# Gate-up products on DVE instead of POOL in a two-layer hybrid decoder trunk, with earlier 1/rms, separate places for weight sums and rebuilt operands spread out

## The chip, the cores and the metric

The kernel runs on one core of one Trainium2 chip. The metric is the device time of one execution in microseconds (us). Most times below come from one profiled execution.

## The reference

Two layers over x of 1024 tokens by 1024 channels, in float32. Each layer adds a token mixer (attention) and then a SwiGLU feed-forward:

```python
h = rms_norm(x, ffn_norm_g[layer])
a = einsum('bsd,df->bsf', h, w_gate)       # d 1024, f 2816
u = einsum('bsd,df->bsf', h, w_up)
x = x + einsum('bsf,fd->bsd', silu(a) * u, w_down)
```

The change touches the first half of the feed-forward alone: `silu(a) * u`.

## The kernel before

Matrix operands are split in a high part (a cast on ACT, L102) and the rest (a subtraction on DVE, L1062 for 128x512, L1055 for 128x1024), and each product is three matmuls (L1129 to L1131).

**Gate and up products.** The 22 tiles of 128 hidden columns go in pairs: 11 batches, b = 0 to 10, in each of two layers. A batch takes seven products, i = 0 to 6, in place of eight, by the Winograd form of Strassen's scheme: a 2x2 block of weights (gate and up, each in the two halves of d_model) by a 2x2 block of activations (halves of d_model, halves of the tokens). Product (b, i) below is product i of batch b. It has two halves, n = 0 and 1, one for each tile of the pair, of 12 matmuls each, so 24 matmuls a product. The left operands are weight blocks and their sums, which `sums_gate` (L1085 to L1087) and L1099 make on POOL from the loaded blocks. The right operands are `self.B[i]`.

**Banks.** Products 0 and 1 of a half add up in the same PSUM bank, as do 2 and 3, 4 and 5. In between, the partial sum is taken: after product 0 by a copy on ACT (L102), after 2 and 4 by an addition on DVE (L1155, L1161). The first matmul of product 1, 3 or 5 waits for that read. Product 6 has a bank of its own.

**What follows a product.** After (b, 5) DVE adds (L1164), ACT applies silu and POOL multiplies (L1166); after (b, 6) DVE adds (L1168) and POOL multiplies (L1169). `hidden` (L1188 to L1191, DVE) then forms the sums of hidden blocks, and SP writes seven blocks to DRAM.

**The start.** 1/rms of the tokens is known late. So batches 0, 1 and 2 (`EARLY = 3`) run products 0 and 1 before it is there, as (0,0), (0,1), (1,0), (1,1), (2,0), (2,1), and then (0,2) to (0,6), (1,2) to (1,6), (2,2) to (2,6). Their first two results are multiplied by 1/rms (`self.rt`, L1151) on DVE, and silu follows, in the step of product 2. The right operands 0 and 1 are dropped after (2,1), and rebuilt from DRAM (L1176, two blocks each after products (2,3) and (2,4)) for batch 3. Batches 3 to 10 run all seven products in order.

**Places and order.** One pool of 44 places of 128x1024 holds split operands (`sr`) and raw tiles (`sf`), another of 11 places of 128x512 the rest (`hf`, `hr`, `raw`). A new tile takes the place that was freed longest ago and waits for that place's last user. The Tile framework fixes the order of each engine's instructions when the kernel is built; each engine then runs its list in order. Operand preparation (`prep_gate`) is asked for 3 or 4 products ahead.

Of the kernel before, what the change touches and what calls it, by code (L numbers as in the profile page):

```python
# [14 lines left out]
AF = mybir.ActivationFunctionType  # L15
ALU = mybir.AluOpType
# [6 lines left out]
TH = 512  # L23
# [93 lines left out]
class Trunk:  # L117
# [960 lines left out]
    def sums_gate(self, b):  # L1078

        p = self.nc.gpsimd  # L1080
        for n in range(2):
            (a11, a21), a22 = (self.raws[b, w][n][:, 0:TH] for w in range(2)), self.raws[b, 1][n][:, TH:2 * TH]
            s1 = self.tmp[b, n] = (self.sf if b == 0 else self.hf).get()
            s1 = s1[:, 0:TH]
            p.tensor_tensor(s1, a21, a22, ALU.add)  # L1085
            p.tensor_tensor(a21, a11, a21, ALU.subtract)
            p.tensor_tensor(a11, s1, a11, ALU.subtract)  # L1087

    def prep_gate(self, b, i):
        p = self.nc.gpsimd  # L1090
        out = []
        for n in range(2):
            g = self.raws[b, 0][n]
            a11, a12 = g[:, 0:TH], g[:, TH:2 * TH]
            if i >= 2:
                u = self.raws[b, 1][n]
                a21, a22 = u[:, 0:TH], u[:, TH:2 * TH]
            if i == 5:
                p.tensor_tensor(a12, a12, a11, ALU.subtract)  # L1099
            out.append(self.split((a11, a12, a11, None, None, a12, None)[i] if i not in (3, 4, 6) else  # L1100
                                  a21 if i == 3 else self.tmp[b, n][:, 0:TH] if i == 4 else a22))
            if i == 4:
                (self.sf if b == 0 else self.hf).put(self.tmp.pop((b, n)))
            if i == 6:
                self.sf.put(g, u)
        due = 0 if (b, i) == (1, 0) else b + 1 if b + 1 < self.EARLY and i == 5 else b if b >= self.EARLY and i == 1 else None
        if due is not None:
            self.sums_gate(due)
        if b + 1 < self.EARLY and i == 3:
            self.take_raw(b + 1, (1,))  # L1110
        elif b + 1 == self.EARLY and i in (4, 6):
            self.take_raw(b + 1, (0,) if i == 4 else (1,))
        elif self.EARLY <= b < self.BATCHES - 1 and i == 1:
            self.take_raw(b + 1)
        return out

    def gate(self, b, i, W):
        nc = self.nc
        if i == 0:
            self.v[b] = [{}, {}]  # L1120
        for n in range(2):
# [12 lines left out]
            v = self.v[b][n]  # L1134
            if i == 0:
                if 0 < b < self.EARLY:
                    t = v["both"] = self.sf.get()
                    v["p"], v["s"] = t[:, 0:TH], t[:, TH:2 * TH]
                else:
                    v["hp"], v["hs"] = self.hf.get(), self.hf.get()  # L1140
                    v["p"], v["s"] = v["hp"][:], v["hs"][:]
                self.S.copy(v["p"], ps)
            elif i == 1:
                if b < self.EARLY:
                    self.S.copy(v["s"], ps)
                else:
                    self.S.activation(v["s"], ps, AF.Silu)
            elif i == 2:
                if b < self.EARLY:
                    for x in ("p", "s"):  # L1150
                        nc.vector.tensor_tensor(v[x], v[x], self.rt[:, 0:TH], ALU.mult)  # L1151
                    self.S.activation(v["s"], v["s"], AF.Silu)
                v["hu"] = self.hf.get()
                v["u"] = v["hu"][:]
                nc.vector.tensor_tensor(v["u"], ps, v["p"], ALU.add)  # L1155
            elif i == 3:
                nc.vector.tensor_tensor(v["p"], ps, v["p"], ALU.add)
            elif i == 4:
                v["hq"] = self.hf.get()
                v["q"] = v["hq"][:]  # L1160
                nc.vector.tensor_tensor(v["q"], ps, v["p"], ALU.add)  # L1161
            elif i == 5:
                u = v["u"]
                nc.vector.tensor_tensor(u, ps, u, ALU.add)  # L1164
                self.S.activation(u, u, AF.Silu)
                nc.gpsimd.tensor_tensor(u, u, v["q"], ALU.mult)  # L1166
            else:
                nc.vector.tensor_tensor(v["p"], ps, v["p"], ALU.add)  # L1168
                nc.gpsimd.tensor_tensor(v["s"], v["s"], v["p"], ALU.mult)  # L1169
        if b == self.BATCHES - 1 or i < 2 and b == self.EARLY - 1:  # L1170
            self.sr.put(*(x for hl in self.B[i] for x in hl))
            self.B[i] = []
        if b == self.EARLY - 1 and i in (3, 4):
            for m in (0, 1) if i == 3 else (2, 3):
                t = self.sf.get()
                nc.sync.dma_start(t[:], self.h_dram[m][:])  # L1176
                self.B[i - 3].append(self.split2(t))
                self.sf.put(t)
        if i == 6:
            self.hidden(b)  # L1180

    def hidden(self, b):

# [364 lines left out]
```

## Time and profile before

| what | us |
|---|---|
| median of 3 runs | 2597.59 |
| range of the 3 runs | 2596.66 to 2600.56 |
| the profiled execution | 2599.55 |
| its span in the profile | 2597.6 |
| gate-up products of layer 0, first L1129 | from 668.9 |

The page of the profile gives busy time by engine. A timeline row gives start, duration, engine, line, operation, output <- inputs, how many rows it merges, and in brackets how long the engine had been idle and what ended that. Names drop buffer numbers: `bk` is a PSUM bank, `sr` a split operand, `sf` and `hf` raw tiles, `rt` 1/rms. `x` in a row of windows is the number of instructions.

### The profile page before, as it was taken

To read this page: it belongs to the slowest core of one execution; us is meant where nothing else is said; L and a number is where in the kernel's file an instruction comes from. 1 tells how busy PE (TensorE), PEld (TensorE's weight loads), DVE (VectorE), ACT (ScalarE), POOL (GpSimd) and SP (SyncE) were. 2 spreads that over 40 slices of the span, in tenths; PEclk is the share of its full clock that TensorE was granted. 3 is DMA by queue.
4 is the path that set the end of the run, shared out by engine and by line. 5 is a ranking of instruction groups with operands and counts; after the bars stand their busy time and mean duration, and the time that the engine had idled before them with its cause. 6 is when DMAs were issued, how large, how long until landed. Compare 5 with 4: busy or idle time off the path is not lost.

```text
span 2597.6 us, 34806 instructions
## 1 busy us (share of the span) xinstructions
PE 2467.1 (95%) x11896; PEld 2021.0 (78%) x11896; DVE 1912.1 (74%) x3303; ACT 1300.8 (50%) x2618; POOL 902.3 (35%) x696
## 2 busy tenths in 40 slices
PE   8898899999989999999999999998998899999999
PEld 7786778777767888888878878876777778888887
DVE  7869958887976655589566687778779666566974
ACT  5646666764732323344456576766565233234352
POOL 4112111121264444366142232323334534443910
PEclk9999999999999999999999999999999999999999
DMA  5323142465323232374333331325531422328462
GB/s 180 91 53 82 36 102 76 116 192 169 109 90 139 96 113 102 131 266 153 111 122 75 83 100 54 98 78 135 178 136 67 150 93 98 110 74 283 126 186 82
DMA packets 148269, 307.50 MB, mean 118 GB/s; under 512 B 18515, under 2 KB 24436, under 8 KB 148092
## 3 DMA queue, kind: packets, MB, share of 16 engines
q1 hardware_dynamic: 148092, 305.28, 37.8%
q8 instruction: 93, 1.52, 0.2%
q14 instruction: 84, 0.69, 0.1%
HBM read 187.74 MB, written 75.53 MB: 101 GB/s over the span
## 4 chain that ended last, share of the span: by engine, by line
PE 64%; DVE 17%; ACT 6%; POOL 5%; issue 5%; DMA 2%; SPq 0%; DVEq 0%; POOLq 0%; ACTq 0%
PE bk L1129 8%; PE bk L1130 8%; PE bk L1131 8%; PE bk L1275 5%; PE bk L1273 5%; PE bk L1274 5%; PE bk L376 4%; PE bk L375 4%; PE bk L377 4%; PE bk L691 4%; PE bk L569 3%; DVE sf L587 3%; PE bk L677 2%; ACT sf L110 2%; DVE sr L1062 2%
## 5 line engine op out<-in xcount | busy, mean ns | idle before, releaser
L102 ACT CAST sr<-sf 128x512 fp32r<-128x512 f32 (+2 forms) x528 | 331.8, 648 | 559.0 <-PE bk L1131 189.0
L1129 PE MATMUL bk<-sr,sr 128*128 128x512 f32 x1232 | 487.8, 396 | 32.2 <-DVE hf L1155 18.0
L1062 DVE TENSOR_TENSOR sr<-sf,sr 128x512 fp32r<-128x512 f32 x430 | 411.2, 963 | 121.5 <-ACT sr L102 119.8
L1131 PE MATMUL bk<-sr,sr 128*128 128x512 f32 x1232 | 483.9, 393 | 3.4 <-DVE sr L1062 3.4
L1130 PE MATMUL bk<-sr,sr 128*128 128x512 f32 x1232 | 484.5, 393 | 0.0
L375 PE MATMUL bk<-sr,sr 128*128 128x512 f32 x768 | 308.2, 402 | 6.7 <-DVE sf L989 3.4
L376 PE MATMUL bk<-sr,sr 128*128 128x512 f32 x768 | 306.5, 399 | 2.4 <-DVE sr L932 2.3
L1129 PEld LDWEIGHTS bk<-sr,sr 128*128 128x128 f32 x1232 | 234.4, 190 | 91.9 <-DVE hf L1155 26.5
L377 PE MATMUL bk<-sr,sr 128*128 128x512 f32 x768 | 305.5, 398 | 0.0
L221 POOL TENSOR_TENSOR sr<-raw,sr 128x512 fp32r<-128x512 f32 (+2 forms) x140 | 191.3, 1383 | 305.9 <-ACT sr L102 174.9
L1131 PEld LDWEIGHTS bk<-sr,sr 128*128 128x128 f32 x1232 | 234.2, 190 | 53.6 <-DVE sr L1062 4.2
L1130 PEld LDWEIGHTS bk<-sr,sr 128*128 128x128 f32 x1232 | 234.5, 190 | 48.3
L1274 PE MATMUL bk<-sr,sr 128*128 128x512 f32 x616 | 239.7, 389 | 0.6 <-DVE sr L1062 0.6
L1273 PE MATMUL bk<-sr,sr 128*128 128x512 f32 x616 | 239.6, 389 | 0.0
L1275 PE MATMUL bk<-sr,sr 128*128 128x512 f32 x616 | 239.6, 389 | 0.0
L102 ACT CAST sr<-hf 128x512 fp32r<-128x512 f32 (+1 forms) x256 | 158.7, 620 | 135.1 <-DMA hf<-td 72.2
L569 PE MATMUL bk<-sr,sr 128*128 128x512 f32 (+2 forms) x768 | 200.4, 359 | 9.2 <-ACT sf L110 6.4
L1062 DVE TENSOR_TENSOR sr<-hf,sr 128x512 fp32r<-128x512 f32 x186 | 188.2, 1021 | 27.4 <-ACT sr L102 26.8
L691 PE MATMUL bk<-hr,sr 128*128 128x512 f32 (+2 forms) x560 | 165.5, 388 | 13.7 <-DVE hr L709 11.0
L375 PEld LDWEIGHTS bk<-sr,sr 128*128 128x128 f32 x768 | 146.1, 190 | 37.3 <-DVE sf L989 5.1
L102 ACT CAST hr<-bk 128x512 fp32r<-128x512 f32 (+2 forms) x240 | 122.5, 525 | 100.8 <-PE bk L677 88.8
L709 DVE TENSOR_TENSOR hr<-bk,hr 128x512 fp32r<-128x512 f32 (+2 forms) x240 | 142.2, 603 | 38.6 <-ACT hr L102 37.1
(203 smaller groups left out, 4917.3 us busy)
## 6 DMA issues: line engine op xcount, KB each, us to landing
hf<-td SPq DMA_DIRECT2D x146, 256.0 KB, 3.1
td<-hf SPq DMA_DIRECT2D x138, 256.0 KB, 2.0
sr<-sr SPq DMA_DIRECT2D x96, 256.0 KB, 3.6
sf<-in_wg_dram SPq DMA_DIRECT2D x44, 512.0 KB, 3.3
sf<-in_wu_dram SPq DMA_DIRECT2D x44, 512.0 KB, 3.3
sf<-in_wd_dram SPq DMA_DIRECT2D x88, 256.0 KB, 5.0
raw<-in_w_dram SPq DMA_DIRECT2D x64, 256.0 KB, 3.0
sr<-sr SPq DMA_DIRECT2D x128, 128.0 KB, 2.3
```

Of the source, the lines that this page charges most:

```text
L102: self.last = self.e.copy(out, in_)
L375: nc.tensor.matmul(ps, WH[k], hH[k], start=first and k == 0, stop=False)
L376: nc.tensor.matmul(ps, WH[k], hL[k], start=False, stop=False)
L377: nc.tensor.matmul(ps, WL[k], hH[k], start=False, stop=last and k == n - 1)
L569: nc.tensor.matmul(b[:, 0:hi - lo], r32(Q[i // 4][:, q]), r32(KK[:, lo:hi]), start=j == 0, stop=j == 1)
L1062: self.nc.vector.tensor_tensor(r32(t[:, TH:2 * TH]), x, t[:, 0:TH], ALU.subtract)
L1129: nc.tensor.matmul(ps, wh, bh, start=i in (0, 2, 4, 6) and j == 0, stop=False, skip_group_check=True)
L1130: nc.tensor.matmul(ps, wh, bl, start=False, stop=False, skip_group_check=True)
L1131: last = nc.tensor.matmul(ps, wl, bh, start=False, stop=j == 3, skip_group_check=True)
L1273: nc.tensor.matmul(ps, wh, bh, start=i in (0, 6, 2, 4) and j == 0, stop=False, skip_group_check=True)
L1274: nc.tensor.matmul(ps, wh, bl, start=False, stop=False, skip_group_check=True)
L1275: nc.tensor.matmul(ps, wl, bh, start=False, stop=j == self.PAIRS - 1, skip_group_check=True)
```

## The change

The two multiplications of `gate` move from POOL to DVE, 88 of them over both layers. The multiplication by 1/rms and the silu of the early batches become `early_r`: batch 0 keeps its step, batches 1 and 2 get it in the step of product 4 of the batch before. The sum s1 of `sums_gate` takes a place of the large pool for all early batches, where only batch 0 did. The four blocks for the right operands of batch 3 are reloaded and split one each after (2,2), (2,3), (2,4) and (2,5).

```diff
@@ sums_gate, and prep_gate where the sum is given back
-            s1 = self.tmp[b, n] = (self.sf if b == 0 else self.hf).get()
+            s1 = self.tmp[b, n] = (self.sf if b < self.EARLY else self.hf).get()
...
-                (self.sf if b == 0 else self.hf).put(self.tmp.pop((b, n)))
+                (self.sf if b < self.EARLY else self.hf).put(self.tmp.pop((b, n)))
@@ gate
             elif i == 2:
-                if b < self.EARLY:
-                    for x in ("p", "s"):
-                        nc.vector.tensor_tensor(v[x], v[x], self.rt[:, 0:TH], ALU.mult)
-                    self.S.activation(v["s"], v["s"], AF.Silu)
+                if b == 0:
+                    self.early_r(v)
...
                 self.S.activation(u, u, AF.Silu)
-                nc.gpsimd.tensor_tensor(u, u, v["q"], ALU.mult)
+                nc.vector.tensor_tensor(u, u, v["q"], ALU.mult)
             else:
                 nc.vector.tensor_tensor(v["p"], ps, v["p"], ALU.add)
-                nc.gpsimd.tensor_tensor(v["s"], v["s"], v["p"], ALU.mult)
+                nc.vector.tensor_tensor(v["s"], v["s"], v["p"], ALU.mult)
+            if i == 4 and b + 1 < self.EARLY:
+                self.early_r(self.v[b + 1][n])
...
-        if b == self.EARLY - 1 and i in (3, 4):
-            for m in (0, 1) if i == 3 else (2, 3):
-                t = self.sf.get()
-                nc.sync.dma_start(t[:], self.h_dram[m][:])
-                self.B[i - 3].append(self.split2(t))
-                self.sf.put(t)
+        if b == self.EARLY - 1 and 2 <= i < 6:
+            t = self.sf.get()
+            nc.sync.dma_start(t[:], self.h_dram[i - 2][:])
+            self.B[i // 2 - 1].append(self.split2(t))
+            self.sf.put(t)
...
+    def early_r(self, v):
+
+        for x in ("p", "s"):
+            self.nc.vector.tensor_tensor(v[x], v[x], self.rt[:, 0:TH], ALU.mult)
+        self.S.activation(v["s"], v["s"], AF.Silu)
```

In the changed kernel the lines are L1153 and L1159 (the additions after products 2 and 4), L1162 and L1166 (after 5 and 6), L1164 and L1167 (the multiplications, now on DVE), L1184 (by 1/rms) and L1193 to L1196 (`hidden`).

The built order of three places of layer 0 follows; layer 1 has the same. The number behind the first letters is the place in the pool, the one behind the underline the tile. First POOL, from the weight sums of batch 1 on (`6977` and `6981` are the two s1). Before:

```order
L1085 TENSOR_TENSOR hf0_6977<-sf40_6881 128x512
L1086 TENSOR_TENSOR sf40_6881<-sf31_6403,sf40_6881 128x512
L1087 TENSOR_TENSOR sf31_6403<-hf0_6977,sf31_6403 128x512
L1085 TENSOR_TENSOR hf1_6981<-sf36_6882 128x512
L1099 TENSOR_TENSOR sf31_6403<-sf31_6403 128x512
L1086 TENSOR_TENSOR sf36_6882<-sf29_6404,sf36_6882 128x512
L1087 TENSOR_TENSOR sf29_6404<-hf1_6981,sf29_6404 128x512
L1099 TENSOR_TENSOR sf29_6404<-sf29_6404 128x512
L1166 TENSOR_TENSOR hf2_6940<-hf2_6940,hf7_7029 128x512
L1166 TENSOR_TENSOR hf3_6957<-hf3_6957,hf8_7043 128x512
L1169 TENSOR_TENSOR hf6_6680<-hf6_6680,hf5_6679 128x512
L1085 TENSOR_TENSOR hf2_7182<-sf2_7088 128x512
```

With the change:

```order
L1085 TENSOR_TENSOR sf43_6977<-sf40_6881 128x512
L1086 TENSOR_TENSOR sf40_6881<-sf31_6403,sf40_6881 128x512
L1087 TENSOR_TENSOR sf31_6403<-sf43_6977,sf31_6403 128x512
L1099 TENSOR_TENSOR sf31_6403<-sf31_6403 128x512
L1085 TENSOR_TENSOR sf39_6981<-sf36_6882 128x512
L1086 TENSOR_TENSOR sf36_6882<-sf29_6404,sf36_6882 128x512
L1087 TENSOR_TENSOR sf29_6404<-sf39_6981,sf29_6404 128x512
L1099 TENSOR_TENSOR sf29_6404<-sf29_6404 128x512
L1085 TENSOR_TENSOR sf35_7178<-sf19_7093 128x512
L1086 TENSOR_TENSOR sf19_7093<-sf30_6407,sf19_7093 128x512
L1087 TENSOR_TENSOR sf30_6407<-sf35_7178,sf30_6407 128x512
L1099 TENSOR_TENSOR sf30_6407<-sf30_6407 128x512
```

The two POOL multiplications of batch 0 (L1166, L1166, L1169) no longer stand between the sums of batch 1 and those of batch 2; the sums of batch 2 follow at once. The first s1 lies in place 43 of the large pool, whose last reader is L1045 on DVE (`sf43_6381`), and the s1 of batch 2 in place 35, which held an operand of (0,6).

Second DVE, from the end of batch 0 (`hidden`, its last additions) to the two additions after (1,2). Before:

```order
L1062 TENSOR_TENSOR sr6_7212<-sf40_6881,sr6_7212 128x512
L1188 TENSOR_TENSOR hf7_7029<-hf2_6940,hf6_6680 128x512
L1168 TENSOR_TENSOR hf4_6694<-bk3_66,hf4_6694 128x512
L1189 TENSOR_TENSOR hf5_6679<-hf3_6957,hf7_7029 128x512
L1062 TENSOR_TENSOR sr7_7215<-sf36_6882,sr7_7215 128x512
L1191 TENSOR_TENSOR hf4_6694<-hf10_6695,hf5_6679 128x512
L1151 TENSOR_TENSOR sf10_6847<-sf10_6847,rt_145 128x512
L1155 TENSOR_TENSOR hf9_7151<-bk4_67,sf25_6761 128x512
L1062 TENSOR_TENSOR sr39_7249<-sf20_6408,sr39_7249 128x512
L1062 TENSOR_TENSOR sr35_7282<-sf22_7087,sr35_7282 128x512
L1062 TENSOR_TENSOR sr43_7246<-sf30_6407,sr43_7246 128x512
L1155 TENSOR_TENSOR hf5_7168<-bk5_68,sf28_6775 128x512
```

With the change:

```order
L1195 TENSOR_TENSOR hf1_7046<-hf3_6957,hf2_6940 128x512
L1167 TENSOR_TENSOR hf6_6680<-hf6_6680,hf5_6679 128x512
L1166 TENSOR_TENSOR hf4_6694<-bk3_66,hf4_6694 128x512
L1193 TENSOR_TENSOR hf0_7029<-hf2_6940,hf6_6680 128x512
L1167 TENSOR_TENSOR hf10_6695<-hf10_6695,hf4_6694 128x512
L1194 TENSOR_TENSOR hf5_6679<-hf3_6957,hf0_7029 128x512
L1062 TENSOR_TENSOR sr7_7175<-sf29_6404,sr7_7175 128x512
L1196 TENSOR_TENSOR hf4_6694<-hf10_6695,hf5_6679 128x512
L1153 TENSOR_TENSOR hf7_7154<-bk4_67,sf25_6761 128x512
L1062 TENSOR_TENSOR sr43_7212<-sf40_6881,sr43_7212 128x512
L1062 TENSOR_TENSOR sr39_7215<-sf36_6882,sr39_7215 128x512
L1153 TENSOR_TENSOR hf8_7168<-bk5_68,sf28_6775 128x512
```

The two multiplications (L1167) are new here, as one more is two rows ahead of the piece. A multiplication by 1/rms (L1151) and three operand splits of batch 2, which stood ahead of one or the other addition after (1,2), are gone from here; two splits of batch 1 stand between the additions instead.

Third ACT, around (3,0), whose bank 0 the copies read. Before:

```order
L102 CAST sr25_7564<-sf31_7333 128x512
L102 CAST sr28_7567<-sf40_7334 128x512
L102 CAST sr10_7570<-sf43_7423 128x512
L102 COPY hf7_7588<-bk0_63 128x512
L102 CAST sr20_7606<-hf1_7509 128x512
L102 CAST sr42_7573<-sf39_7424 128x512
```

With the change:

```order
L102 CAST sr35_7564<-sf29_7339 128x512
L102 CAST sr41_7567<-sf36_7340 128x512
L102 COPY hf1_7588<-bk0_63 128x512
L102 CAST sr39_7606<-hf10_7509 128x512
L102 CAST sr10_7570<-sf17_7423 128x512
L102 COPY hf9_7603<-bk1_64 128x512
```

The copy of the first half of (3,0) stands ahead of the cast of `7423`, which reuses a place that `hidden` of batch 2 still sends to DRAM; before, it stood behind that cast.

## Rows read from the trace of the kernel before

**Rows 1.** Page, part 1: engine, busy us, share of the span, instructions.
```profile
PE 2467.1 (95%) x11896; PEld 2021.0 (78%) x11896; DVE 1912.1 (74%) x3303; ACT 1300.8 (50%) x2618; POOL 902.3 (35%) x696
```

**Rows 2.** 50 us windows: busy us (instructions) of PE, PEld, DVE, ACT, POOL; clock; DMA.
```profile
700.00:750.00 50.00, 41.83 (x175) 33.41 (x173) 44.05 (x51) 20.29 (x33) 28.07 (x15) 0.97 0.23 74
750.00:800.00 50.00, 43.62 (x180) 34.99 (x180) 33.97 (x41) 14.79 (x22) 24.16 (x16) 0.93 0.40 138
850.00:900.00 50.00, 49.99 (x221) 41.04 (x220) 31.27 (x38) 15.17 (x26) 24.91 (x18) 1.00 0.31 112
```

**Rows 3.** Timeline of PE, layer 0: matmuls that waited; wait and releaser in brackets.
```profile
729.07 0.50 PE L1129 MATMUL bk<-sr,sr 128*128 128x512 f32 x1 [2.91 <-DVE hf L1161]
753.36 0.79 PE L1129 MATMUL bk<-sr,sr 128*128 128x512 f32 x1 [6.92 <-DVE hf L1155]
759.76 0.50 PE L1129 MATMUL bk<-sr,sr 128*128 128x512 f32 x1 [1.44 <-DVE hf L1155]
800.95 0.50 PE L1129 MATMUL bk<-sr,sr 128*128 128x512 f32 x1 [2.23 <-DVE hf L1161]
819.15 0.80 PE L1129 MATMUL bk<-sr,sr 128*128 128x512 f32 x1 [2.65 <-ACT hf L102]
```

**Rows 4.** Timeline of PE, the same matmuls in layer 1.
```profile
1993.48 0.80 PE L1129 MATMUL bk<-sr,sr 128*128 128x512 f32 x1 [2.91 <-DVE hf L1161]
2017.78 0.79 PE L1129 MATMUL bk<-sr,sr 128*128 128x512 f32 x1 [7.17 <-DVE hf L1155]
2024.18 0.50 PE L1129 MATMUL bk<-sr,sr 128*128 128x512 f32 x1 [0.91 <-DVE hf L1155]
2064.23 0.50 PE L1129 MATMUL bk<-sr,sr 128*128 128x512 f32 x1 [1.08 <-DVE hf L1161]
2080.42 0.50 PE L1129 MATMUL bk<-sr,sr 128*128 128x512 f32 x1 [2.28 <-ACT hf L102]
```

**Rows 5.** Windows of 4 us behind the wait that ends at 729.07.
```profile
728.00:732.00 4.00, 2.94 (x9) 2.34 (x10) 2.21 (x4) 1.24 (x3) 3.84 (x3) 0.78 0.00 0
732.00:736.00 4.00, 4.00 (x15) 3.18 (x15) 3.97 (x6) 3.24 (x6) 0.90 (x2) 0.79 0.00 0
```

**Rows 6.** Timeline of POOL, DVE and ACT, layer 0, ahead of 729.07.
```profile
716.74 6.87 POOL L1086 TENSOR_TENSOR sf<-sf,sf 128x512 f32<-128x512 f32 x1
...
716.63 2.34 DVE L1045 TENSOR_TENSOR sf<-sf,sf 128x1024 f32<-128x1024 f32 x2
...
722.37 1.27 DVE L1157 TENSOR_TENSOR hf<-bk,hf 128x512 f32<-128x512 f32 x2
...
726.60 1.80 DVE L1062 TENSOR_TENSOR sr<-sf,sr 128x512 fp32r<-128x512 f32 x1 [2.36 <-ACT sr L102]
...
735.10 0.63 ACT L110 ACTIVATE hf<-hf 128x512 f32<-128x512 f32 x1 [0.49 <-DVE hf L1164]
```

**Rows 7.** Timeline of DVE, layer 0, ahead of the wait that ends at 753.36.
```profile
749.30 1.73 DVE L1191 TENSOR_TENSOR hf<-hf,hf 128x512 f32<-128x512 f32 x1 [1.15 <-POOL hf L1169]
750.95 1.75 DVE L1151 TENSOR_TENSOR sf<-sf,rt 128x512 f32<-128x512 f32 x1
752.62 0.68 DVE L1155 TENSOR_TENSOR hf<-bk,sf 128x512 f32<-128x512 f32 x1
```

**Rows 8.** DVE and POOL in the down projection: two timeline rows, then a 50 us window.
```profile
1160.89 1.77 DVE L1062 TENSOR_TENSOR sr<-hf,sr 128x512 fp32r<-128x512 f32 x1
...
1160.49 1.62 POOL L1234 TENSOR_TENSOR sf<-sf,sf 128x512 f32<-128x512 f32 x1
...
1150.00:1200.00 50.00, 50.00 (x222) 41.38 (x222) 50.00 (x31) 20.13 (x37) 48.82 (x31) 1.00 0.34 102
```

**Rows 9.** Lines L1166 and L1188: count, duration ns min/median/max.
```profile
L1166 POOL TENSOR_TENSOR hf<-hf,hf x44: 1272/1296/1612, 735.8 to 2380.9; 128x512 f32<-128x512 f32 x44
...
L1188 DVE TENSOR_TENSOR hf<-hf,hf x18: 677/1226/1766, 743.9 to 2386.1; 128x512 f32<-128x512 f32 x18
```

**Rows 10.** Timeline of PE, a later batch of layer 0.
```profile
1026.53 0.50 PE L1129 MATMUL bk<-sr,sr 128*128 128x512 f32 x1 [0.32 <-DVE hf L1155]
```

## The prediction, made before the change was run

> **What bounds the kernel now.** I read the page first, then windows over the gate-up products, then the timeline of PE there, and last the queues of the engines that PE waited for. PE is busy for 95% of the span [rows 1], so only time in which it stands, or runs at less than its clock, can be won. The windows show where that is: from 850 us on 221 matmuls start in 50 us, which is 0.226 us each and 5.43 us for a product of 24; the two windows ahead of it hold 175 and 180 [rows 2]. So batches 3 to 10 run without a gap, and the early batches do not. In layer 0 five waits stand there, of 2.91, 6.92, 1.44, 2.23 and 2.65 us [rows 3], and the same five in layer 1, of 2.91, 7.17, 0.91, 1.08 and 2.28 [rows 4]. By the order of PE's matmuls the waiting ones are the first of (0,5), of (1,3) first half, of (1,3) second half, of (2,5) and of (3,1). Four of the five wait for an addition on DVE that must read a bank, the last for a copy on ACT.
>
> A wait costs more than itself where the clock falls behind it. After 729.07 the granted clock is 0.78 and 0.79 of full speed over two windows, a time at 1.2 GHz in place of 2.4; 24 matmuls take from 729.07 to 736, 6.93 us where 5.43 would do [rows 2, 3, 5]. I price a fall at 1.5 us.
>
> **What holds DVE and POOL.** Where both have additions with two inputs in SBUF queued, they take turns: 31 and 31 in 50 us, 1.61 us for a pair, while a DVE row reads 1.77 and a POOL row 1.62, waiting included [rows 8]. Alone, the same operations take 0.68 (two in a row 1.27, so 0.60 each in a stream) and 1.30 [rows 6, 9]. There is an exception, and it matters below: the POOL addition at 716.74 lasted 6.87 us, and ended 1.24 us after DVE turned to operands in PSUM at 722.37; five DVE instructions had gone ahead of it [rows 6]. The Trainium skill (SBUF — State Buffer, section "Who interferes with whom") says that a DVE instruction with two SBUF inputs contends with a GpSimd instruction that reads SBUF, and that issue order decides who blocks. The turns agree with that; the 6.87 us do not. By that rule alone the time would be my forecast; by the exception it would be the second case below.
>
> **The change part by part.**
>
> *The multiplications.* POOL loses 88 of 1.30 us, some 114 us, none of it in PE's way by itself. DVE gains 88 of 0.60, 53 us. In a batch of 7 x 5.43 = 38 us that is 2.4 us, and DVE stands twice more for a silu (0.63 on ACT, about 0.7 with the hand-over) [rows 6, 9], 3.8 us in all. DVE is busy for 31.27 of 50 us there, 14 us free a batch [rows 2], and today it also waits 1.15 us for a POOL multiplication twice a batch [rows 7]. So from batch 3 on I cost this at nothing; the cover is that idle time. If it were gone, the next addition that reads a bank would be late: one is already, by 0.32 [rows 10].
>
> *Wait at (0,5), 729.07.* The s1 of batch 1 now lies in place 43, which L1045 reads until 716.63 + 1.17 = 717.8; before, L1085 was done when L1086 was queued at 716.74. The first POOL addition to get through ends at 723.6 as before [rows 6], but it is now L1085, and L1086 and L1087 follow one addition later. DVE's split at 726.60 stands behind ACT's cast, which stands behind the cast of L1087's result. So this wait ends one POOL addition later, 1.3 us, at 730.4. In the queue of ACT the cast is also third instead of second behind L1087, 0.5 us; that falls into the same POOL addition. Bounds: nothing, if POOL gets in at 717.8 without a queue, and 1.9, if the two add.
>
> *Wait at (1,3), 753.36.* PE stands from 753.36 - 6.92 = 746.4; with the 1.3 us, from 747.7. Before, DVE was here behind a POOL multiplication (1.15), a blocked L1191 (1.73) and a blocked multiplication by 1/rms (1.75) [rows 7]. The first and the last of these are gone from this place. In their stead nine DVE instructions with two SBUF inputs (splits, three multiplications, `hidden`) meet the eight POOL additions of batch 2's sums, which now follow directly. These can begin when the first half of (0,6) is done, since the s1 takes an operand's place: 32 matmuls after 730.4, 6.93 + 8 x 0.226 = 8.7, so at about 739.3. Eight turns with POOL's share of about 1.1 and DVE's of 0.6, 1.70 together (the two rows there last 1.73 and 1.75), end at 752.9 [rows 7]; two more DVE instructions and the addition itself (0.68) bring 754.9. So the wait stays, 7.2 us, and ends 1.5 us later than before. Without turns DVE needs 12 x 0.60 from 739.9, is there at 747.1, and no wait is left. I take the first value, since in this same stretch of the trace DVE's rows read 1.73 and 1.75 [rows 7].
>
> *Second half of (1,3).* The three splits of batch 2 that stood between the two additions are gone; the two in their place have their operands ready. The waits of 1.44 and 0.91 go [rows 3, 4].
>
> *Wait at (2,5).* The sums of batch 3 and the reloaded operands meet here. With one reload a step, the split of 1.2 us stands ahead of the first addition and none between the two. The second addition has 2.7 us (12 matmuls) after its bank is written, and two DVE instructions and one blocked turn, 1.70 + 0.60, before it. I let 2.23 and 1.08 go; each can come back by a blocked turn.
>
> *Wait at (3,1).* The copy on ACT stood behind a cast that waits for `hidden` of batch 2; now it stands ahead of it. The 2.65 and 2.28 go, for that reason alone.
>
> *Falls.* Behind (2,5) in layer 0 and behind (3,1) in both layers the clock no longer falls: three at 1.5 us. Four DMAs that were issued as two and two are now one a step on SP, each behind the writes of `hidden`; the last is split three products before it is used, so I cost them at nothing.
>
> **Sum.** Waits: 1.44 + 2.23 + 2.65 + 0.91 + 1.08 + 2.28 = 10.6. Falls: 4.5. Against that 1.5 a layer, 3.0. Net 12.1 us faster. The profiled execution took 2599.55, which is 1.96 above the median of the runs; 2597.59 - 12.1 = **2585.5**.
>
> **Rivals.**
>
> *The wait at (1,3) goes too.* DVE streams past POOL as it did at 716.74. For it: DVE has no gap from 735 on. Against it: the turns in rows 7 and 8. The two waits of 7.2 and 7.4 go, with two falls; the first half of (1,3) ran from 753.36 to 758.32 (759.76 less 1.44) where 12 matmuls need 2.7 [rows 3], so 2.2 each. 2585.5 - 14.6 - 4.4 = 2566.5; half of the turns would give about 2576.
>
> *Nothing to be measured.* The change does not free DVE: the waits at (2,5) and (3,1) return, as multiplications that wait for silu and blocked turns fill what the spread took out. Then the 10.6 and 4.5 stay partly or wholly, and the 3.0 come on top: half gives 2593, all 2600.6.
>
> *Slower.* In each of the 16 later batches the products and silu waits push the addition after product 2 (L1153) past PE's turn. It is 0.32 late at one place already [rows 10]. The added 3.8 less the removed 2 x 1.15 leaves 1.5 us that would have to arrive there. Batches 3 to 10 of two layers are 16, and 16 x 1.5 = 24, so 2609.5. It decides from the point where DVE's 14 idle us a batch lie wholly behind the last bank read; PE waits for this bank only some 20 us after the products, which speaks against it.
>
> **How the numbers follow.** The forecast has 0.55, and its own range is 2579 to 2592; the (1,3) wait gone in part or whole 0.21; nothing to be measured 0.16; slower 0.08. A measurement of this kernel can tell 0.2%, 5.2 us, from no change. Faster by more: 0.55 less a little, 0.21, and a little of the third, 0.75. Within: 0.16. Slower: 0.09. The range reaches from the second case, 2565, to half of the third, 2596; left out are the slower case and the worse half of the third.
>
> **What would show it.** In the changed kernel the wait at (0,5) should read about 4.2 us in both layers and end on DVE L1159; the one at (1,3) about 7 us, on L1153, with DVE rows of 1.7 us between 739 and 753 and POOL rows L1085 to L1099 beside them. Behind it no wait over 0.5 us up to batch 3, and windows of 220 matmuls from 765 on. The forecast is wrong if the wait at (1,3) is under 3 us, if a wait stands at (2,5) or (3,1), or if the windows of the later batches fall under 219.

## The result, and the profile after

The changed kernel takes 2576.81 us (median of 6 runs, 2575.85 to 2578.96), the kernel before 2598.64 (6 runs): a ratio of 0.9921, 95% interval 0.9911 to 0.9931, which is 20.5 us faster (the two medians are 21.8 apart; ratios here and below are taken against runs of the kernel before in the same session). The forecast was 2585.5 and the range 2565 to 2596. The sign and what happens at the five places were right; the gain was 1.7 times the 12.1 us that were forecast. The time lies below the 2579 to 2592 that the forecast named as its own, and inside the wider range. One execution of e5, told below, read 7397 us; its ratio leaves that one out, and no trace shows the cause.

The page, part 1, of the changed kernel: engine, busy us, share of the span, instructions.

```profile
PE 2456.4 (95%) x11896; PEld 2016.9 (78%) x11896; DVE 1946.7 (76%) x3391; ACT 1303.1 (51%) x2618; POOL 764.3 (30%) x608
```

Beside [rows 1], DVE has 88 instructions more and POOL 88 fewer, and PE is busy 10.7 us less with the same matmuls. The mean granted clock rose from 0.985 to 0.988, so fewer of them ran at the lower clock. The windows of the changed kernel, to be read beside [rows 2] (the one of 800 to 850 not shown there read 189 matmuls before):

```profile
700.00:750.00 50.00, 39.93 (x164) 31.84 (x162) 45.46 (x50) 19.75 (x31) 27.52 (x16) 0.93 0.21 74
750.00:800.00 50.00, 47.63 (x201) 39.24 (x202) 38.55 (x54) 15.24 (x22) 13.85 (x9) 0.93 0.47 161
800.00:850.00 50.00, 49.76 (x220) 40.92 (x219) 36.04 (x47) 16.21 (x28) 16.75 (x12) 1.00 0.34 124
850.00:900.00 50.00, 50.00 (x223) 41.32 (x222) 32.13 (x41) 16.83 (x29) 16.00 (x12) 1.00 0.23 79
```

The first window is worse than before (164 matmuls for 175), the second and third are better, and the last, where nothing was to be won, holds 223 for 221. The waits of PE in the changed kernel, layer 0 and then layer 1:

```profile
728.00 0.80 PE L1129 MATMUL bk<-sr,sr 128*128 128x512 f32 x1 [4.39 <-DVE hf L1159]
752.37 0.80 PE L1129 MATMUL bk<-sr,sr 128*128 128x512 f32 x1 [6.36 <-DVE hf L1153]
...
1980.46 0.80 PE L1129 MATMUL bk<-sr,sr 128*128 128x512 f32 x1 [4.39 <-DVE hf L1159]
2004.93 0.80 PE L1129 MATMUL bk<-sr,sr 128*128 128x512 f32 x1 [6.36 <-DVE hf L1153]
```

Of the five waits of [rows 3, 4] two stand, at (0,5) and (1,3); the other three are gone in both layers.

The order of PE's matmuls is the same in both kernels, so the trace can be cut at the start of the same matmul. The next table gives such stretches for the two kernels and for the experiments told below, in us, layer 0 / layer 1. "Early" runs from the first matmul of (0,0) to that of (4,0), "late" from there to the last gate-up matmul. The stretch from (0,5) begins four matmuls ahead of the one that waits, so the wait at (0,5) is in the first stretch and the one at (1,3) in the second. In e11 and e12 some matmuls between (0,5) and (1,4) stand in another order, so their first three stretches can be off by a matmul or two; early and late are not touched by that.

```
                               (0,5)-(1,2)    (1,2)-(1,4)    (1,4)-(2,6)    (2,6)-(4,0)    early            late             median
before                         15.75 / 15.51  21.77 / 22.03  42.80 / 40.06  48.05 / 47.70  184.54 / 181.44  268.49 / 269.21  2598.64
changed                        17.86 / 17.97  19.61 / 19.68  38.08 / 38.08  44.04 / 44.13  175.75 / 175.99  266.35 / 266.37  2576.81
e1 products back on POOL       17.67 / 17.87  23.25 / 23.31  39.74 / 39.74  48.25 / 48.18  185.08 / 185.23  268.48 / 268.53  2601.48
e2 s1 in small places          15.61 / 14.06  13.20 / 16.34  43.30 / 40.07  44.85 / 43.91  173.12 / 170.42  266.44 / 266.45  2571.41
e3 s1 of batch 1 small         15.55 / 14.12  19.13 / 22.10  38.08 / 38.08  44.14 / 43.99  173.03 / 174.31  266.55 / 266.45  2574.65
e4 reload two and two          17.98 / 17.15  19.69 / 19.14  39.72 / 38.83  43.96 / 44.66  177.47 / 175.82  266.44 / 266.45  2581.86
e5 products alone              15.69 / 15.75  14.41 / 14.41  43.76 / 43.56  45.51 / 43.88  176.71 / 173.62  266.43 / 266.46  2575.06
e6 early 1/rms back            17.66 / 17.64  19.01 / 19.04  38.08 / 38.08  43.97 / 43.90  174.89 / 174.68  266.45 / 266.39  2577.52
e7 s1 of batch 2 small         17.17 / 17.17  15.79 / 15.75  39.30 / 38.97  44.63 / 43.90  173.05 / 171.82  266.45 / 266.44  2572.50
e8 e7 + ready cast first       10.88 / 10.88  22.93 / 22.69  38.64 / 38.87  44.09 / 44.01  172.71 / 172.50  266.35 / 266.35  2571.86
e9 e2 + ready cast first       10.88 / 10.88  19.67 / 19.61  42.20 / 44.01  44.26 / 44.41  173.16 / 174.95  266.35 / 266.35  2579.94
e10 product after 5 on POOL    17.67 / 17.77  22.23 / 22.28  38.37 / 38.38  46.03 / 45.21  180.45 / 179.65  266.46 / 266.45  2587.48
e11 e8 + half the sums on DVE  14.95 / 13.89  12.35 / 14.99  40.65 / 39.07  44.17 / 43.75  168.26 / 167.72  266.51 / 266.47  2564.92
e12 e11 + early 1/rms back     15.25 / 14.91  12.05 / 12.37  41.48 / 40.71  44.63 / 43.75  169.53 / 167.76  266.48 / 266.47  2563.39
```

Without a wait the first four would be 10.88, 10.88, 38.08 and 43.52 us (48, 48, 168 and 192 matmuls of 0.2267). The changed kernel gained 8.8 and 5.4 us in the early stretches and 2.1 and 2.8 in the late ones, 19.2 us in all. The rest of the 22.7 us between the two spans lies outside the gate-up products, and so outside the change: 2.5 us ahead of those of layer 0, whose first matmul starts at 668.91 before and 666.40 after, and 1.0 between the two layers' products. That start lies between 664.84 and 670.18 in the experiments, so a median of theirs can differ by a few us without a cause in these stretches.

### The profile page after: what moved, and what is told of

The parts are those of the page before. It is cut to its first block, busy times and chain, and to the rows that moved or that the text cites. A ratio compares the mean times of both kernels' runs of the same rounds, so it can differ in the third digit from the quotient of the medians.

```text
span 2574.9 us, 34805 instructions
## 1 busy us (share of the span) xinstructions
PE 2456.4 (95%) x11896; PEld 2016.9 (78%) x11896; DVE 1946.7 (76%) x3391; ACT 1303.1 (51%) x2618; POOL 764.3 (30%) x608
## 4 chain that ended last, share of the span: by engine, by line
PE 67%; DVE 19%; ACT 6%; issue 4%; DMA 2%; POOL 2%; SPq 0%; DVEq 0%; ACTq 0%; POOLq 0%
PE bk L1129 9%; PE bk L1130 9%; PE bk L1131 9%; PE bk L1278 5%; PE bk L1279 5%; PE bk L1280 5%; PE bk L376 4%; PE bk L375 4%; PE bk L377 4%; PE bk L691 4%; PE bk L569 3%; DVE sf L587 3%; PE bk L677 2%; DVE sr L1062 2%; ACT sf L110 2%
## 5 line engine op out<-in xcount | busy, mean ns | idle before, releaser
L102 ACT CAST sr<-sf 128x512 fp32r<-128x512 f32 (+2 forms) x536 | 337.0, 648 | 572.3 <-PE bk L1131 235.3
L1062 DVE TENSOR_TENSOR sr<-sf,sr 128x512 fp32r<-128x512 f32 x438 | 400.5, 923 | 143.9 <-ACT sr L102 142.6
L1062 DVE TENSOR_TENSOR sr<-hf,sr 128x512 fp32r<-128x512 f32 x178 | 180.2, 1016 | 35.7 <-ACT sr L102 34.9
```

Source lines behind the costliest of these rows:

```text
L102: self.last = self.e.copy(out, in_)
L1062: self.nc.vector.tensor_tensor(r32(t[:, TH:2 * TH]), x, t[:, 0:TH], ALU.subtract)
```

## The experiments

**e1, the products back on POOL.** The changed kernel with

```diff
-                nc.vector.tensor_tensor(u, u, v["q"], ALU.mult)
+                nc.gpsimd.tensor_tensor(u, u, v["q"], ALU.mult)
...
-                nc.vector.tensor_tensor(v["s"], v["s"], v["p"], ALU.mult)
+                nc.gpsimd.tensor_tensor(v["s"], v["s"], v["p"], ALU.mult)
```

> The changed kernel with the 88 multiplications of gate and up put back on POOL; its other three parts stay. Theory A (the multiplications carry most of the gain): a batch from 4 on takes 38.39 us again where the changed kernel takes 38.09, which is 5 us over 16 batches; the copy on ACT stands behind the cast again in the built order, so the wait at (3,1) is back with 2.3 to 2.7 us in both layers, 7.6 us with what follows it. Median 2586 to 2593. Theory B (the other three parts carry the gain, the multiplications are neutral): 38.09 us a batch, no wait at (3,1), median 2576 to 2579.

2601.48 us, ratio to the kernel before 1.0021 (1.0011 to 1.0030): A in its places, with a median 8.5 us above A's range. Without the multiplications the other three parts lose. The waits of PE in layer 0:

```profile
755.61 0.79 PE L1129 MATMUL bk<-sr,sr 128*128 128x512 f32 x1 [10.34 <-DVE hf L1153]
786.21 0.47 PE L1129 MATMUL bk<-sr,sr 128*128 128x512 f32 x1 [1.38 <-DVE hf L1153]
816.49 0.50 PE L1129 MATMUL bk<-sr,sr 128*128 128x512 f32 x1 [2.80 <-ACT hf L102]
```

The last is the wait at (3,1), back with the order on ACT: the copy runs at 815.86, behind the cast at 815.34. The first is what A missed: here POOL's multiplications stand among the sums of batch 2, and DVE waits for one of them, as its rows ahead of 755.61 show, with POOL's below.

```profile
751.55 1.73 DVE L1196 TENSOR_TENSOR hf<-hf,hf 128x512 f32<-128x512 f32 x1 [2.38 <-POOL hf L1167]
753.21 1.74 DVE L1184 TENSOR_TENSOR sf<-sf,rt 128x512 f32<-128x512 f32 x1
...
748.70 1.60 POOL L1086 TENSOR_TENSOR sf<-sf,sf 128x512 f32<-128x512 f32 x1
750.26 1.26 POOL L1167 TENSOR_TENSOR hf<-hf,hf 128x512 f32<-128x512 f32 x1
```

There is no wait at (2,5), so the spread reload alone is enough there.

**e5, the products alone.** The kernel before with the two lines of e1 the other way round, and nothing else.

> The kernel before with the 88 multiplications moved to DVE, and nothing else. Putting them back on POOL in the changed kernel cost 22.9 us in the stages it touches: 9.3 and 9.2 in the early batches of the two layers, 4.3 in the later ones. Theory A (the multiplications carry the gain by themselves; with s1 in the small places POOL's additions of batch 2 wait for hidden of batch 0): 38.09 us a batch from batch 4 on, no wait at (3,1), a wait of under 3 us at (1,3) first half, the wait at (2,5) stays between 1 and 2.3 us. Median 2572 to 2580. Theory B (the multiplications pay only together with the other three parts): a wait of 6 to 8 us at (1,3), median 2584 to 2592.

2575.06 us, ratio 0.9915 (0.9895 to 0.9935): A. This one part gives the whole gain. The first half of (1,3) doesn't wait; its second half does, 3.23 us, and (1,5) 3.35. The wait that A left at (2,5) is all but gone too (0.41 and 0.24 us lost in the stretch from (2,4) to (2,6)), though the reload is two and two here: the multiplications alone are nearly enough there as well.

**e10, one of the two products.** The changed kernel with only the first of e1's two lines back on POOL.

> The changed kernel with only the multiplication after product 5 back on POOL; the one after product 6 stays on DVE. Theory A (in the later batches it is the multiplication after product 6 that counts: with it on POOL the second half's weight sums of the next batch begin 5.7 us into the batch in place of before it, meet DVE's splits, and the addition after product 2 is 0.3 us late): 38.09 us a batch stays, and the copy stays ahead of the cast, so no wait at (3,1). POOL has two more additions at (1,3), which makes the wait there 7 to 9 us. Median 2577 to 2584. Theory B (any multiplication on POOL brings the 0.3 us back): 38.39 us a batch, median 2582 to 2589.

2587.48 us, ratio 0.9954 (0.9938 to 0.9971). In the late stretch A is right: 266.46 us, and the wait at (1,3) is 8.51 us, as A said. But the early stretch is dearer than A put it, 180.45 for 175.75, and the median lies in B's range. So the 0.3 us a batch come with the multiplication after product 6 on POOL (no run has that one alone there), and both cost turns at (1,3): 6.36, 8.51 and 10.34 us with none, one and two of them there.

Where the 0.3 us come from is in the rows of batch 4. In the kernel before, POOL's multiplication of batch 3, a sum of batch 4 behind it, and the DVE rows beside them:

```profile
858.19 1.67 POOL L1169 TENSOR_TENSOR hf<-hf,hf 128x512 f32<-128x512 f32 x1 [1.23 <-DVE hf L1168]
...
859.89 0.69 DVE L1191 TENSOR_TENSOR hf<-hf,hf 128x512 f32<-128x512 f32 x1 [1.18 <-POOL hf L1169]
...
861.27 1.67 POOL L1085 TENSOR_TENSOR hf<-sf 128x512 f32<-128x512 f32 x1 [1.41 <-DVE sr L1062]
863.02 1.78 POOL L1086 TENSOR_TENSOR sf<-sf,sf 128x512 f32<-128x512 f32 x1
...
864.33 1.01 DVE L1062 TENSOR_TENSOR sr<-sf,sr 128x512 fp32r<-128x512 f32 x1 [0.69 <-ACT sr L102]
...
871.92 0.68 DVE L1155 TENSOR_TENSOR hf<-bk,hf 128x512 f32<-128x512 f32 x1
...
872.26 0.39 PE L1131 MATMUL bk<-sr,sr 128*128 128x512 f32 x1
872.66 0.50 PE L1129 MATMUL bk<-sr,sr 128*128 128x512 f32 x1
```

and in the changed kernel, where batch 4 begins at 842.14 and not at 853.45:

```profile
849.08 1.68 POOL L1086 TENSOR_TENSOR sf<-sf,sf 128x512 f32<-128x512 f32 x1
...
853.02 0.69 DVE L1062 TENSOR_TENSOR sr<-sf,sr 128x512 fp32r<-128x512 f32 x1 [0.69 <-ACT sr L102]
...
860.29 0.69 DVE L1153 TENSOR_TENSOR hf<-bk,hf 128x512 f32<-128x512 f32 x1
```

Before, DVE waited for the multiplication (859.89), POOL's next sum waited for a split of DVE behind that (861.27), and so the sum at 863.02 ran until 864.80 and held up the split (1.01 for 0.69); everything behind was 0.32 later, and the addition ended at 872.60, when PE was due at 872.49 (872.26 and one matmul). After, the sum ends at 850.76, 2.3 us ahead of the split, and the addition is 0.2 us ahead of PE. The gap of 872.66 is too small to be marked as a wait; it shows as 0.40 us between two starts, where 0.23 is usual. Batches 4 to 9 of both layers have such a gap at product 3; batch 10 has none.

**e2, e3, e7: where s1 lies.** In the changed kernel

```diff
-            s1 = self.tmp[b, n] = (self.sf if b < self.EARLY else self.hf).get()
+            s1 = self.tmp[b, n] = (self.sf if b == 0 else self.hf).get()
```

and the same where it is given back; in e3 the condition is `b in (0, 2)`, in e7 `b in (0, 1)`.

> The changed kernel with s1 of batches 1 and 2 back in places of the small pool. By the built order s1 of batch 1 no longer waits for L1045, and s1 of batch 2 waits for places that hidden of batch 0 still reads, so POOL's eight additions of batch 2 begin some 5 us later. Theory A (the wait at (1,3) is made by these eight additions, which take turns with DVE between 738 and 751 us): the wait at (0,5) is back at 2.9 us (from 4.4), and the wait at (1,3) falls from 6.4 to under 2 us, median 2556 to 2564. Theory B (at (1,3) DVE's own twelve instructions and the silu are what is late): (0,5) 2.9 us, (1,3) 6 to 7.5 us, median 2571 to 2575.

> The changed kernel with s1 of batch 1 alone in a place of the small pool; batches 0 and 2 keep places of the large one. Theory A (the growth of the wait at (0,5) from 2.9 to 4.4 us is the wait of L1085 for place 43; the wait at (1,3) hangs on the additions of batch 2, which begin when the first half of (0,6) is done, as in the changed kernel): (0,5) 2.9 us, (1,3) 6 to 7.5 us, both layers, median 2571 to 2575. Theory B (the growth at (0,5) has another cause on DVE or ACT): (0,5) 4.4 us, median 2576 to 2578.

> The changed kernel with s1 of batch 2 alone in places of the small pool. By the built order one s1 finds a free place at once, so that its four additions can begin some 6 us earlier than in the changed kernel, and the other waits for a block of hidden to be sent, so that its four begin after about 747. Theory A (the wait at (1,3) is as long as POOL's additions lie between 738 and 751 us): the wait at (0,5) stays 4.4 us, the wait at (1,3) falls from 6.4 to 1 to 3.5 us, median 2565 to 2573. Theory B (DVE's own queue is late): 6 to 7 us at (1,3), median 2576 to 2578.

e2: 2571.41, ratio 0.9907 (0.9890 to 0.9923). e3: 2574.65, ratio 0.9918 (0.9903 to 0.9932). e7: 2572.50, ratio 0.9909 (0.9889 to 0.9928). In e2 and e3 the wait at (0,5) is 2.89 to 2.94 us, in e7 4.38: place 43 is what made it grow. At (1,3) the wait falls in e2 and e7, and stays in e3, as A said; in layer 1 of e2 1.24 and 2.04 us are left there. The medians of e3 and e7 lie in A's ranges, that of e2 in B's. e2's DVE and POOL rows in layer 0:

```profile
741.40 0.68 DVE L1193 TENSOR_TENSOR hf<-hf,hf 128x512 f32<-128x512 f32 x1
742.00 0.68 DVE L1167 TENSOR_TENSOR hf<-hf,hf 128x512 f32<-128x512 f32 x1
742.60 0.69 DVE L1194 TENSOR_TENSOR hf<-hf,hf 128x512 f32<-128x512 f32 x1
743.21 0.69 DVE L1062 TENSOR_TENSOR sr<-sf,sr 128x512 fp32r<-128x512 f32 x1
743.81 0.68 DVE L1196 TENSOR_TENSOR hf<-hf,hf 128x512 f32<-128x512 f32 x1
744.41 0.68 DVE L1153 TENSOR_TENSOR hf<-bk,sf 128x512 f32<-128x512 f32 x1
...
742.16 3.48 POOL L1085 TENSOR_TENSOR hf<-sf 128x512 f32<-128x512 f32 x1 [10.08 <-DVE hf L1193]
745.72 1.62 POOL L1086 TENSOR_TENSOR sf<-sf,sf 128x512 f32<-128x512 f32 x1
```

Up to this L1153, DVE has the same operations in the same order as in the changed kernel, whose rows are

```profile
744.95 1.77 DVE L1167 TENSOR_TENSOR hf<-hf,hf 128x512 f32<-128x512 f32 x1
746.63 1.74 DVE L1194 TENSOR_TENSOR hf<-hf,hf 128x512 f32<-128x512 f32 x1
748.30 1.74 DVE L1062 TENSOR_TENSOR sr<-sf,sr 128x512 fp32r<-128x512 f32 x1
749.97 1.74 DVE L1196 TENSOR_TENSOR hf<-hf,hf 128x512 f32<-128x512 f32 x1
751.63 0.68 DVE L1153 TENSOR_TENSOR hf<-bk,sf 128x512 f32<-128x512 f32 x1
...
746.24 1.59 POOL L1086 TENSOR_TENSOR sf<-sf,sf 128x512 f32<-128x512 f32 x1
747.91 1.59 POOL L1087 TENSOR_TENSOR sf<-sf,sf 128x512 f32<-128x512 f32 x1
```

The same instructions are 0.60 us apart in one kernel and 1.67 in the other; the difference is POOL, which in e2 has nothing ready until 742.16, and whose first addition then gets no turn ahead of L1153. But e2's sums are then late elsewhere, and the time is above what A gave:

```profile
750.23 0.50 PE L1129 MATMUL bk<-sr,sr 128*128 128x512 f32 x1 [1.97 <-DVE hf L1153]
761.99 0.55 PE L1129 MATMUL bk<-sr,sr 128*128 128x512 f32 x1 [3.31 <-DVE hf L1159]
```

e7 has its wait at (1,3) at 2.98 and 2.97 us and little else. In e3 the wait is 6.31 and 8.35 us, the second above what was expected. In that layer POOL's sums of batch 2 follow those of batch 1 without a pause until 1997.89, and DVE's rows with two SBUF inputs beside them are 1.2 to 1.8 us long; from 1998.37 to the addition at 2003.78 they are 0.60 apart again. So the turns were lost earlier there. Why the wait is 2 us longer than in layer 0 no run tells.

**e4 and e6, the other two parts undone.** e4 puts back the reload of two blocks after (2,3) and two after (2,4); e6 puts back

```diff
-                if b == 0:
+                if b < self.EARLY:
                     self.early_r(v)
...
-            if i == 4 and b + 1 < self.EARLY:
-                self.early_r(self.v[b + 1][n])
```

> The changed kernel with the four blocks for batch 3 reloaded two and two again, after (2,3) and (2,4). Theory A (the wait at (2,5) went because no 128x1024 split stands between the two additions any more): 1 to 2.5 us of wait are back at (2,5) in both layers, median 2580 to 2584. Theory B (it went because POOL and DVE are earlier there, with no multiplication on POOL): no wait over 0.5 us at (2,5), median 2576 to 2578.

> The changed kernel with the multiplications by 1/rms of batches 1 and 2 back in the step of their own product 2. Theory A (on DVE the place of these four matters where they meet POOL's additions or stand ahead of a bank read): one or two of them, 1.7 us each, stand ahead of the additions after (1,2) again; the waits at (1,3) are 2 to 4 us longer in sum and a wait of 0.3 to 1.4 us is back at (2,3). Median 2582 to 2587. Theory B (they are hidden in either place): 2576 to 2578.

e4: 2581.86, ratio 0.9945 (0.9931 to 0.9960). A wait at (2,5) is back, with 1.26 us at the first half in layer 0 and 0.50 at the second in layer 1. The median lies in A's range, but the waits are short of A's in layer 1, and only 1.7 us of the 5.0 lie in the stretches of the table. e5, with the same reload and no such wait, speaks for B. So the place of the reload counts, but it is not the whole cause. e6: 2577.52, ratio 0.9926 (0.9912 to 0.9941): B. Its wait at (1,3) is even shorter, 5.45 and 5.50 us.

**e8, e9: a cast that was ready.** Of the two waits left, the one at (0,5) has a cause on ACT: the cast of (0,6)'s second operand, long ready, stands behind two casts that wait for POOL's L1087, and DVE stands idle for it ahead of the addition (changed kernel):

```profile
725.95 1.40 DVE L1062 TENSOR_TENSOR sr<-sf,sr 128x512 fp32r<-128x512 f32 x1 [4.22 <-ACT sr L102]
```

In e7's and e2's kernels the casts of (1,2) and (1,3) are put behind it (`self.cast` is the last cast that `split` issued; in step 8 that is the one of (0,6)):

```diff
+            if m in (9, 10):
+                with self.tc.issue_after(behind):
+                    prep_to(m + 3)
             prep_to(m + (3 if m < 7 * self.EARLY else 4 if s < 0 else 5))
+            if m == 8:
+                behind = self.cast.ins
```

> The kernel of the run with s1 of batch 2 alone in small places, and beside that the casts on ACT of the operands of (1,2) and (1,3) are ordered behind the cast of the second operand of (0,6), which is ready long before them. Theory A (the wait at (0,5) is that ready cast standing in ACT's queue behind two casts that wait for L1087): the wait at (0,5) falls from 4.4 to under 0.5 us, and the idle 4.2 us of DVE ahead of it go. PE is 4.4 us earlier at (1,3), where DVE's list is as long as before but starts earlier: the wait there grows from 3.0 to 3 to 6 us. Median 2564 to 2571. Theory B (POOL's 5.64 us addition sets the pace, so the time only moves): (0,5) under 0.5, but 7 to 8 us at (1,2) or (1,3), median 2571 to 2574.

> The kernel with s1 of batches 1 and 2 in small places, with the same order on ACT as the run beside it (here one cast of (1,3) still stands ahead of one of (1,2)). Theory A: the wait at (0,5) falls from 2.9 to under 0.5 us in both layers; some of it comes back at (1,3), where the wait was 2.0 us and 1.2 and 2.0 us. Median 2564 to 2570. Theory B (the time only moves): the waits at (1,3) and (1,5) grow by the 2.9 us, median 2570 to 2573.

e8: 2571.86, ratio 0.9897 (0.9882 to 0.9912). e9: 2579.94, ratio 0.9929 (0.9914 to 0.9944). The wait at (0,5) is gone in both, so the cause was right. The gain is not there: B, though the wait of e8 at (1,3) is longer than B's 7 to 8 us and the median of e9 lies above both ranges. In e8, PE, then DVE and POOL (the lines are one further down):

```profile
748.77 0.77 PE L1130 MATMUL bk<-sr,sr 128*128 128x512 f32 x1 [9.53 <-DVE hf L1154]
...
732.18 1.24 DVE L1063 TENSOR_TENSOR sr<-sf,sr 128x512 fp32r<-128x512 f32 x1 [4.57 <-ACT sr L102]
...
715.62 5.63 POOL L1086 TENSOR_TENSOR sf<-sf 128x512 f32<-128x512 f32 x1 [39.77 <-DVE sf L1045]
```

DVE's idle time has only moved, to the cast of the second half of (1,2), which waits for the seventh of POOL's eight sums. They begin at 715.62, and the first of them loses 4.3 us to DVE's stream. In e9 the waits at (1,3) and (1,5) grew in sum by more than what was taken away, and it is slower than e2, by 4.6 us in the stretches of the table and 8.5 in the median; the rest lies outside them.

**e11, e12: fewer sums on POOL.** So e8 with the sums of the second tile of batch 1 on DVE:

```diff
+            p = self.nc.vector if n == 1 and b in (1,) else self.nc.gpsimd
             p.tensor_tensor(s1, a21, a22, ALU.add)
```

and the same ahead of the subtraction for product 5; e12 is e11 with e6's edit.

> The kernel of the run with the ready cast first, and the four sums of the second tile of batch 1 (three of the weight sums, and the subtraction for product 5) on DVE in place of POOL. Theory A (what bounds the stretch from 714 to 749 us is POOL's chain of sums, begun late behind DVE's stream, and the turns that DVE loses to it): POOL has four additions less there, DVE 2.4 us more of its own and four lost turns of 1.1 us less, and its wait of 4.6 us for a cast behind POOL's sums goes. The addition for (1,3) comes 5 to 6.5 us earlier, the wait there is 3 to 4.5 us in place of 9.5, no wait at (0,5). Median 2557 to 2564. Theory B (DVE's list is what bounds it): the wait at (1,3) stays at 8 us or more, median 2569 to 2573.

> The same kernel with the multiplications by 1/rms of batches 1 and 2 back in the step of their own product 2. Theory A (where they stand makes little difference, as putting them back alone changed the median by under 1 us): within 3 us of the run beside it. Theory B (out of the crowded stretch they free two of DVE's operations there, and the waits at (1,3) fall by 1 to 2.5 us a layer): 3 to 6 us faster than the run beside it.

e11: 2564.92, ratio 0.9873 (0.9856 to 0.9890). e12: 2563.39, ratio 0.9868 (0.9853 to 0.9882). e11 bears A out in kind: the wait at (1,3) falls, to 1.15 and 2.19 us, which is below A's 3 to 4.5. But a wait of 2.15 us for a cast behind POOL's sums is left at (0,5), where A had none, another stands at (1,5), and the median lies 0.9 us above A's range. e12 is A. In e11, layer 0, the waits at (1,3) and (1,5) read:

```profile
745.57 0.50 PE L1132 MATMUL bk<-sr,sr 128*128 128x512 f32 x1 [1.15 <-DVE hf L1156]
758.58 0.47 PE L1132 MATMUL bk<-sr,sr 128*128 128x512 f32 x1 [2.04 <-DVE hf L1162]
```

Both beat the two kernels; e12 is 34 us faster than the one before. DVE is busy there for all of 50 us in e12:

```profile
700.00:750.00 50.00, 45.10 (x189) 35.83 (x188) 50.00 (x58) 21.22 (x33) 23.26 (x12) 0.97 0.28 96
```

## Why the prediction was right, and where its size was off

The forecast by its places, and what the same stretches of the two traces give (us gained, layer 0 / layer 1; the forecast has the wait, and 1.5 more where a fall of the clock goes with it):

```
                                        forecast        measured
up to the end of the wait at (1,3)      -1.5  / -1.5    -1.52 / -1.63
from there to (1,4)                      1.44 /  0.91    1.59 /  1.54
(1,4) to (2,4)                           0    /  0       0.59 /  0.59
(2,4) to (2,6), wait at (2,5)            3.73 /  1.08    4.13 /  1.39
(2,6) to (4,0), wait at (3,1)            4.15 /  3.78    4.01 /  3.57
batches 4 to 10                          0    /  0       2.14 /  2.84
sum                                          12.1            19.2
```

- **(0,5).** Right in place, size and cause. 4.2 us were forecast and 4.39 measured, in both layers. e3 shows the cause.
- **(1,3).** Right: an end at 754.9, which is 86.0 us after the first gate-up matmul; it came after 85.97 (752.37 less 666.40). That it is right to 0.1 us is luck: POOL's sums began 71.5 us after that matmul and not 70.4, but took 0.4 less, and 1.1 us of DVE work stood behind them in place of 2.0. The wait itself is 6.36 for 7.2, as PE came later. The turns were the reason to take this value and not the rival's, and e2 and e7 show that they are the cause. The rival in which the wait goes was wrong for this order, but it is what e2 and e5 do once POOL's sums begin later.
- **(1,3) second half, (2,5), (3,1).** Gone, as forecast. At (2,5) the reload is one cause and the multiplications another: with either part alone the wait is gone or nearly so (e1, e5), and e4 brings a part of it back. For (3,1) I named the order on ACT and not what makes it: the multiplications, as e1 brings the wait back and e5 alone removes it.
- **Falls.** 1.5 us each was a little low. At (2,5) in layer 0 4.13 us came back for a wait of 2.23, so 1.9; at (3,1) in layer 1 4.18 for 2.28 up to (3,2), again 1.9, before 0.61 were lost to a new short wait at (3,3). Behind (0,5) it was 1.96 before and 2.59 after.
- **The step that failed.** "So from batch 3 on I cost this at nothing." I asked only whether DVE would be late, and bounded that by its idle time. The reading that batches 3 to 10 run without a gap was wrong. There was a gain in it, 5.0 us, by POOL: the multiplication after product 6 had pushed the next batch's sums into DVE's splits. I had one row of it, [rows 10], read it as a sign that there was no slack, and did not ask what made that addition late. The gap at (2,3) was left out too: 0.30 us before, where DVE's L1191 had waited 1.19 for the same multiplication, and 0.59 a layer with the slow matmuls behind it. e1 brings it back with 1.38.
- **The rest.** The 19.2 us of the stretches and the 20.5 of the ratio agree: its interval is 17.9 to 23.1 us. The wide range reached down to 2565 for a rival in which the wait at (1,3) goes, which did not happen; the time came in there by the 5.0 us that the forecast left out, the 1.2 at (2,3) and the falls.
- **What I did not see at all.** The four parts are not of one kind. The multiplications alone give the whole gain; with them in place the spread reload adds 1.6 us in the early stretches (e4: 353.3 for 351.7), the earlier 1/rms gains nothing (e6: 0.7 us in the median, and 2.2 the other way in the early stretches), and the places for s1 take away (without them e2 is 8.2 us shorter in the early stretches and 5.4 in the median, though the intervals of the two ratios overlap). The sum had the sign right for the four together, and says little of any one.

On the turns the Trainium skill (SBUF — State Buffer, section "Who interferes with whom") has a DVE instruction with two SBUF inputs contend with a GpSimd instruction that reads SBUF. These runs agree: 0.60 and 1.67 us between the same instructions in e2 and the changed kernel. The Trainium skill (Perfetto Trace Analysis, section "Optimizing Scalar/DVE Operations") warns that moving work between these two engines might not help, because they share a read port. These runs agree, and more: putting 88 multiplications on POOL cost 24.7 us (e1's median less that of the changed kernel).

## What to carry to other kernels

When an engine is off the critical path but shares something with one that is on it, cost a moved instruction at both: what it takes on the engine it goes to, and which of the other's instructions it no longer stands beside or ahead of. Look at gaps in PE too short to be marked as waits if they come once in every batch, and follow one back to its first late instruction. Undo the parts of a change one by one; one of four carried this one, and one of four seems to have cost time.

## What the hardware did that I had not expected

A POOL addition that becomes ready while DVE runs additions with two SBUF inputs back to back is mostly served next, and then it is DVE's following row that is long. In the feed-forward of the changed kernel 16 of POOL's weight sums became ready so, after an idle time of POOL, and were served next; two were not, one a layer. One of the 16:

```profile
737.93 1.43 POOL L1085 TENSOR_TENSOR sf<-sf 128x512 f32<-128x512 f32 x1 [6.08 <-PE bk L1131]
...
738.13 1.78 DVE L1164 TENSOR_TENSOR hf<-hf,hf 128x512 f32<-128x512 f32 x1
```

The others are passed over by one DVE instruction after another. Two more cases show it beside [rows 6], each a POOL row with the DVE row that reads a PSUM operand, at whose start the addition got in: of the changed kernel,

```profile
715.45 5.64 POOL L1085 TENSOR_TENSOR sf<-sf 128x512 f32<-128x512 f32 x1 [39.77 <-DVE sf L1045]
...
719.85 1.28 DVE L1155 TENSOR_TENSOR hf<-bk,hf 128x512 f32<-128x512 f32 x2
```

and of e11:

```profile
716.55 6.23 POOL L1087 TENSOR_TENSOR sf<-sf 128x512 f32<-128x512 f32 x1 [39.77 <-DVE sf L1045]
...
721.56 0.68 DVE L1158 TENSOR_TENSOR hf<-bk,hf 128x512 f32<-128x512 f32 x1
```

From the start of the DVE row to the end of the POOL row it is 1.24 us, 1.22, and 1.23 in e2 (745.64 less 744.41); in [rows 6] it was 1.24. What sets these apart from the addition at 737.93 no run here tells. It is not that they stood alone: the one of [rows 6] came 0.08 us behind another POOL addition:

```profile
713.76 2.90 POOL L1085 TENSOR_TENSOR hf<-sf 128x512 f32<-128x512 f32 x1 [35.56 <-DMA sf<-in_wu_dram]
```
